# A fixed instruction order in one stage, y tiles split in place, and eight ordering edges on loads and weight splits in a decoder-layer kernel

## The chip, the cores and the metric

One core of a Trainium2 chip runs the kernel. The metric is device time in microseconds (us) from start to end of the program; the runs before the change gave 1829.06, 1829.22 and 1833.78, so their median is 1829.22. The engines are TensorE (PE; PEld is its weight load), VectorE (DVE), ScalarE (ACT), GpSimd (POOL) and SyncE (SP, which here issues nearly all loads).

## What is computed

One layer of a decoder trunk for a sequence of 1024 tokens and a width of 1024. Three kinds of head work side by side on the same normalized input, each is gated by a sigmoid of its own columns, the gated sum goes through W_out, and a feed-forward block with a short convolution follows. Cut to its core:

```python
h = rms_norm(x); P = h @ W_in
A = rwkv7(P)              # 8 heads x 64; per token: S = S*w + (S @ -kk)(kk*a) + v k ; y = S @ r
B = stick_breaking(P)     # 8 heads x 64, causal
M = cross_attention(P, mem)   # 4 heads x 128, 256 memory tokens
x += sum_b(sigmoid(G_b) * (branch_b @ W_br[b])) @ W_out
x += conv_ffn(rms_norm(x))
```

## The kernel before

**Numbers.** Every large product is made of three matmuls: each float32 operand is split into a high part that TensorE takes as it is and a low part (the rest), and `mm3` adds hi x hi, hi x lo and lo x hi into one PSUM bank. A weight tile of 128 x 1024 is loaded by SP into a `wr` slot (`load_w`, 2 slots), ACT copies it to `wh` (L81), and POOL subtracts to get `wl` (L82). The activations of a branch are split alike: `load_y` loads four 128 x 1024 tiles of branch output from DRAM (`yd`) into `w4` tiles, ACT writes `yhi` (L1129), DVE writes the low part into a tile of the tag `A` (L1130). The tag `w4` has 3 slots, and `A` has 4.

**Stages in time.** Input norm and transposes; the preparation of the recurrence (`rwkv_prep`); stick-breaking attention (`sb_attn`, 325 to 650 us); cross attention (`mem_attn`, to some 770 us); the recurrence (`stage2`, 805 to 1005 us) followed by its `group_norm`; the last branch (`branch_last`, to 1091 us); `out_proj`; and the feed-forward block, from 1187 us on.

**Two streams.** From the first preparation to the group norm, `weave` takes turns between a stage and a stream of items called the pump: projections of the input (`proj_item`: 8 steps of six matmuls into two PSUM banks of the tag `mm`, which has 4 banks) and products of a finished branch with its output weights (`branch_item`: 4 such steps). In the recurrence one step of `stage2` is followed by 2.08 steps of the pump. The pump does branch 1 (stick-breaking) in the first part of the recurrence and branch 2 (memory) in the second; between them stands one gate projection whose steps 3 to 6 call the four splits of `load_y`.

**A step of the recurrence.** `stage2` walks 16 chunks of 64 tokens, each in three steps. Step one multiplies the state and adds; DVE copies the result out of four `g` banks (`ys<-g`, L530, four copies). Step two solves; ACT copies eight results (`qk<-g`, L538). Step three makes the outputs and the new state; DVE updates the state (L548, four operations), ACT copies eight outputs (L550). The next step of the stage on PE needs these results, and its own banks. A part of the normalization (`norm_part`) is mixed in: sums on DVE (L573), squares on ACT (L580, `jk`), the scaling on DVE (L589).

**What sets the order.** A list scheduler orders each engine's instructions by their estimated readiness. `pinned` marks an instruction to be kept in program order among the marked ones of the whole program. Not marked before: the sums of `norm_part`, and the DVE operations that empty a branch item's banks (L1162), the copies that empty a projection's banks (L755, L797, L806) and the weight splits. SP issues its loads in one order, each waiting for its slot. At the end of a projection or a branch item `fin` or the emptying of banks comes in the same step as the last matmuls.

**The last branch.** `branch_last` loads for each of eight output tiles a gate (`at<-gsd`) and the sum so far (`w<-mrd`, L1198), and multiplies and adds on DVE (L1220, L1225). The eight weight tiles of W_out are loaded by `load_wo`, four within that loop, four behind it.

Of the kernel before, what the change touches and what calls it, by code (L numbers as in the profile page):

```python
# [50 lines left out]
class Trunk:  # L51
    def __init__(self, ctx, tc, I, out):
        self.ctx, self.tc, self.nc, self.I, self.out = ctx, tc, tc.nc, I, out
        self.uid = 0
        self.pin = False
# [19 lines left out]
    def load_w(self, src):  # L75
        raw = self.pool_wt.tile([128, 1024], F32, name=self.nm("wr"), tag="wr", bufs=2)
        self.nc.sync.dma_start(raw, src)
        return raw

    def split_raw(self, raw, hi, lo):  # L80
        self.nc.scalar.activation(hi, raw, AF.Copy)  # L81
        self.nc.gpsimd.tensor_tensor(lo, raw, hi.bitcast(F32), ALU.subtract)  # L82
        return hi, lo

# [23 lines left out]
    def pinned(self, ins):  # L108
        if self.pin:
            self.tc.keep_in_program_order(ins)  # L110

# [455 lines left out]
    def norm_part(self, g0, g1):  # L567
# [4 lines left out]
        for p, y in enumerate(ys):  # L572
            nc.vector.tensor_reduce(nm[:, p * nh : (p + 1) * nh], y.rearrange("p (g i) -> p g i", i=64), AX.X, ALU.add)  # L573
        nc.vector.tensor_scalar(nm[:, : 4 * nh], nm[:, : 4 * nh], -1.0 / 64, None, ALU.mult)
# [135 lines left out]
    def proj_item(self, src, fin, hook={}):  # L710
        w = self.split_w(src)
        yield
        out = [self.ps("mm"), self.ps("mm")]
        for k in range(8):
            ks = slice(k * 128, (k + 1) * 128)
            self.mm3(out, [a[:, ks] for a in w], self.xin(k), k == 0, k == 7)
            if k == 4:
                self.close_gates()
            if k in hook:
                hook[k]()  # L720
            if k < 7:
                yield
        fin(out)
        yield
# [24 lines left out]
    def gate_item(self, b, d, hook={}, keep=None):  # L749
        nc = self.nc  # L750

        def fin(pp):
            g = self.t4()
            for h in range(2):
                nc.scalar.activation(g[:, h * 512 : (h + 1) * 512], pp[h], AF.Copy)  # L755
# [13 lines left out]
    def sb_qk(self, p, out):  # L769
# [4 lines left out]
        def k_fin(pp):  # L774
            kr, sq = self.t4(), self.t4()
            for h in range(2):
                nc.scalar.activation(kr[:, h * 512 : (h + 1) * 512], pp[h], AF.Copy)
# [25 lines left out]
        def q_fin(pp):  # L803
            qr, sq = self.t4(), self.t4()
            for h in range(2):
                nc.scalar.activation(qr[:, h * 512 : (h + 1) * 512], pp[h], AF.Copy)  # L806
# [19 lines left out]
        hooks = {1: lambda: k_split(1), 3: q_ss, 4: lambda: q_split(0), 6: lambda: q_split(1)}  # L826
# [199 lines left out]
    def mem_q(self, h, out, hook):  # L1026
# [3 lines left out]
        def fin(pp):  # L1030
            sq = self.t4()
            qhi, qlo = self.t4("qk", F32R), self.t4("qk", F32R)
            for i in range(2):
                hs = slice(i * 512, (i + 1) * 512)
                self.pinned(nc.scalar.activation(qhi[:, hs], pp[i], AF.Copy, scale=self.par("memq")))
                self.pinned(nc.scalar.activation(sq[:, hs], pp[i], AF.Square))
# [74 lines left out]
    def load_y(self, b, st):  # L1111
# [4 lines left out]
        def load():  # L1116
            y = self.t4("w4")
            nc.sync.dma_start(y, self.yd[b, len(ys)])
            ys.append(y)

        def first():
            for _ in range(3):
                load()

        def split(k):
            if k == 0:
                st["hi"] = self.pool_a.tile([128, 4, 1024], F32R, name=self.nm("yhi"), tag="inst")
            hi, lo, y = st["hi"][:, k], self.t4("A", F32R), ys[k]
            self.pinned(nc.scalar.activation(hi, y, AF.Copy))  # L1129
            self.pinned(nc.vector.tensor_tensor(lo, y, hi.bitcast(F32), ALU.subtract))  # L1130
            out.append((hi, lo))
            if k == 0:
                load()
# [7 lines left out]
    def branch_item(self, b, d, st, first):  # L1141
# [11 lines left out]
        for k in range(4):  # L1153
# [3 lines left out]
            if k < 3:  # L1157
                yield
        g = st.pop(("g", d))
        for h in range(2):  # L1160
            hs = slice(h * 512, (h + 1) * 512)
            nc.vector.tensor_tensor(g[:, hs], pp[h], g[:, hs], ALU.mult)  # L1162
# [3 lines left out]
        yield  # L1166
# [11 lines left out]
    def load_wo(self, k):  # L1178
        slots = ["qk"] * 4 + ["at"] * 4 + ["it", "sp"] + ["qk"] * 4 + ["at"] * 2
        hl = [self.pool_l.tile([128, 1024], F32R, name="wo_sp", tag="sp", bufs=1) if s == "sp" else self.t4(s, F32R) for s in slots[2 * k : 2 * k + 2]]  # L1180
        self.wo.append(self.split_raw(self.load_w(self.I["w_out"][k]), *hl))

    def branch_last(self):
# [10 lines left out]
        def load(d):  # L1194
            if d < 8:
                go[d] = self.t4("at"), self.t4()
                nc.sync.dma_start(go[d][0], self.gsd[0, d])
                nc.sync.dma_start(go[d][1], self.mrd[d])  # L1198
# [587 lines left out]
    def run(self):  # L1786
# [62 lines left out]
        pace[0] = 8  # L1849
        need("sb0")  # L1850
# [3 lines left out]
        need("mem")  # L1854
        st2 = self.stage2()
        next(st2)
        need("y1")
        self.weave(st2, pump, 2.08, 0)
        self.weave(self.group_norm(), pump, 1.0, 0)
        drain(pump)  # L1860
# [80 lines left out]
```

## Time and profile before

| quantity | value |
|---|---|
| median of three runs | 1829.22 us |
| time of the profiled execution | 1831.78 us |
| its span, first to last instruction | 1830.0 us |
| PE busy | 1785.9 us |
| DVE / ACT / POOL busy | 1191.1 / 881.9 / 771.2 us |
| PE in 767 to 1025 us (recurrence) | 249.85 us of 258.00 |
| PE in 325 to 640 us (stick-breaking) | 310.85 us of 315.00 |

PE is busy nearly all of the time, so the table is to be read from what is missing on PE: the gaps between its instructions, and the stretches in which the profile shows a granted clock below 1. In the rows of a window view the columns are the window, its length, the busy time (and number of instructions) of PE, PEld, DVE, ACT and POOL, the granted clock, the share of the DMA engines that is busy, and GB/s. A row of waits says which engine and line waited for which, the sum in us, how many times, and the longest. A row of the timeline has the start, the time taken, the engine, the line, the operation and its tiles, and in brackets the idle time before it and what ended it. In the list of DMA issues the last number is the median time from issue to landing in us.

### The profile page before, as it was taken

What the parts mean: (1) busy time and instruction counts of PE and PEld (TensorE: products, weight loads), DVE (VectorE), ACT (ScalarE), POOL (GpSimd) and SP (SyncE); (2) the same over time, 40 slices, a digit from 0 to 9 for tenths busy, and PEclk for the clock granted to TensorE, in tenths of its full rate; (3) what the DMA queues carried; (4) which work ended last, traced back from release to release, by engine and by line L of the source; (5) the groups of instructions that cost most, each with busy time, mean ns of one, the idle gap of its engine ahead of it and who ended that gap; (6) DMA issues with size and microseconds to landing.
All of it is one profiled execution on the core that took longest, in us unless ns stands there. A gap on an engine that the chain in (4) does not pass through costs nothing.

```text
span 1830.0 us, 27430 instructions
## 1 busy us (share of the span) xinstructions
PE 1785.9 (98%) x10468; PEld 1445.7 (79%) x10468; DVE 1191.1 (65%) x1659; ACT 881.9 (48%) x1665; POOL 771.2 (42%) x441
## 2 busy tenths in 40 slices
PE   8999999999999999999899999989999999999999
PEld 6777778878788888787677878868888888888887
DVE  5657664988987514333444793597776777785497
ACT  5443342564666635534456443464454444545443
POOL 2322343232222452122233341376776767645454
PEclk9999999999999999999899999999999999999999
DMA  4255466111112351467665463323232232386475
GB/s 181 58 173 184 151 201 204 50 41 52 56 45 84 112 144 53 164 211 257 222 244 185 163 251 104 114 70 115 101 117 88 95 118 104 123 291 247 144 236 202
DMA packets 120613, 263.39 MB, mean 144 GB/s; under 512 B 28313, under 2 KB 40857, under 8 KB 120354
## 3 DMA queue, kind: packets, MB, share of 16 engines
q1 hardware_dynamic: 82722, 194.76, 32.6%
q10 hardware_dynamic: 33984, 54.27, 8.1%
q0 software_dynamic: 3776, 12.62, 2.2%
q8 instruction: 82, 1.34, 0.3%
q14 instruction: 49, 0.40, 0.1%
HBM read 180.04 MB, written 81.53 MB: 143 GB/s over the span
## 4 chain that ended last, share of the span: by engine, by line
PE 83%; DVE 8%; issue 3%; ACT 3%; POOL 2%; DMA 1%; ACTq 0%; SPq 0%; DVEq 0%; POOLq 0%
PE mm L113 67%; PE g L113 12%; PE g L106 3%; POOL dw L1677 1%; DVE qk L379 1%; DVE qk L381 1%; DVE it L462 1%; DVE BT L1318 1%; DVE inst L464 0%; DVE at L854 0%; DVE mg L1232 0%; DMA w<-yd 0%; ACT wh L81 0%; POOL wl L82 0%; DVE qk L382 0%
## 5 line engine op out<-in xcount | busy, mean ns | idle before, releaser
L82 POOL TENSOR_TENSOR wl<-wr,wh 128x1024 fp32r<-128x1024 f32 x77 | 196.8, 2557 | 473.4 <-ACT wh L81 469.7
L113 PE MATMUL mm<-xhi,wh 128*128 128x512 f32 x784 | 264.6, 418 | 9.4 <-ACT xhi L182 7.5
L113 PE MATMUL mm<-xlo,wh 128*128 128x512 f32 x784 | 245.8, 395 | 0.9 <-DVE xlo L183 0.9
L113 PE MATMUL mm<-xhi,wl 128*128 128x512 f32 x784 | 244.3, 393 | 0.3 <-POOL wl L82 0.2
L113 PEld LDWEIGHTS mm<-xlo,wh 128*128 128x128 f32 x784 | 148.8, 190 | 34.5 <-DVE xlo L183 1.6
L113 PEld LDWEIGHTS mm<-xhi,wl 128*128 128x128 f32 x784 | 148.3, 189 | 34.0 <-POOL wl L82 1.2
L113 PEld LDWEIGHTS mm<-xhi,wh 128*128 128x128 f32 x784 | 137.7, 191 | 39.5 <-issue 9.1
L81 ACT ACTIVATE wh<-wr 128x1024 fp32r<-128x1024 f32 x77 | 81.4, 1058 | 147.0 <-PE mm L113 85.4
L113 PE MATMUL mm<-dw,da 128*128 128x512 f32 x528 | 121.2, 390 | 0.0
L113 PE MATMUL mm<-BT,l 128*128 128x512 f32 x504 | 117.7, 390 | 0.0
L113 PEld LDWEIGHTS mm<-dw,da 128*128 128x128 f32 x528 | 99.0, 188 | 21.6 <-DVE da L1676 1.2
L1677 POOL TENSOR_TENSOR dw<-draw,dw 128x512 fp32r<-128x512 f32 x55 | 81.9, 1499 | 79.1 <-ACT dw L1675 76.4
L113 PE MATMUL mm<-BT,wh 128*128 128x512 f32 x352 | 109.2, 391 | 2.9 <-DVE BT L1318 2.9
L854 DVE TENSOR_TENSOR_SCAN at<-at,at 128x128 f32<-128x128 f32 (+3 forms) x64 | 93.4, 1460 | 26.6 <-ACT at L848 26.4
L113 PEld LDWEIGHTS mm<-BT,l 128*128 128x128 f32 x504 | 94.7, 188 | 19.6
L113 PE MATMUL mm<-B,wh 128*128 128x512 f32 x352 | 108.7, 390 | 1.5 <-DVE p L1508 1.5
L1676 DVE TENSOR_TENSOR da<-draw,da 128x512 fp32r<-128x512 f32 x77 | 67.0, 877 | 49.5 <-ACT da L1674 49.1
L1409 POOL TENSOR_TENSOR l<-it,l 128x1024 fp32r<-128x1024 f32 x21 | 51.6, 2458 | 95.5 <-ACT l L1408 95.5
L113 PE MATMUL g<-dw,da 128*128 128x512 f32 x396 | 90.6, 390 | 0.3 <-POOL dw L1677 0.3
L1674 ACT ACTIVATE da<-draw 128x512 fp32r<-128x512 f32 x77 | 48.3, 628 | 80.8 <-PE mm L113 30.9
L113 PEld LDWEIGHTS g<-dw,da 128*128 128x128 f32 x396 | 74.3, 188 | 16.1 <-POOL dw L1677 0.8
L756 DVE TENSOR_TENSOR w<-w,rbc 128x1024 f32<-128x1024 f32 x24 | 49.8, 2074 | 56.8 <-ACT w L755 55.0
(329 smaller groups left out, 3996.5 us busy)
## 6 DMA issues: line engine op xcount, KB each, us to landing
wr<-in_w_in_dram SPq DMA_DIRECT2D x50, 512.0 KB, 3.6
draw<-actd SPq DMA_DIRECT2D x77, 256.0 KB, 3.5
at<-scr SPq DMA_DIRECT2D x28, 512.0 KB, 5.8
draw<-in_w_down_dram SPq DMA_DIRECT2D x55, 256.0 KB, 4.7
rw<-in_w_up_dram SPq DMA_DIRECT2D x22, 512.0 KB, 3.5
actd<-gall ACTq DMA_DIRECT2D x44, 256.0 KB, 3.3
gsd<-w ACTq DMA_DIRECT2D x20, 512.0 KB, 2.8
wr<-in_w_up_dram SPq DMA_DIRECT2D x20, 512.0 KB, 3.6
```

What stands on the lines that cost most here:

```text
L81: self.nc.scalar.activation(hi, raw, AF.Copy)
L82: self.nc.gpsimd.tensor_tensor(lo, raw, hi.bitcast(F32), ALU.subtract)
L106: self.pinned(self.nc.tensor.transpose(out, in_, self.ident[:n, :n]))
L113: self.pinned(self.nc.tensor.matmul(*a, **k))
L379: nc.vector.tensor_tensor(bk4[q, :, first ^ h2], self.c8(x[q, hs]), self.c8(Q[q, hs]), ALU.mult)
L381: nc.vector.scalar_tensor_tensor(ra4[:, :, 1, 1:64], self.c8(P[:, hs])[:, :, 0:63], -1.0, self.c8(kk[:, hs])[:, :, 1:64], ALU.mult, ALU.mult)
L756: nc.vector.tensor_tensor(g, g, self.rbc, ALU.mult)
L854: self.pinned(nc.vector.tensor_tensor_scan(sn[:, :W][:, ::-1], sn[:, :W][:, ::-1], self.smask[:, 1024 - W :][:, ::-1], 1.0, ALU.mult, ALU. ...
L1409: keep(eng.tensor_tensor(lo, src, hi.bitcast(F32), ALU.subtract))
L1674: self.pinned(nc.scalar.activation(A[:, 0], a, AF.Copy))
L1676: self.pinned(nc.vector.tensor_tensor(A[:, 1], a, A[:, 0].bitcast(F32), ALU.subtract))
L1677: nc.gpsimd.tensor_tensor(Wt[:, 1], w, Wt[:, 0].bitcast(F32), ALU.subtract)
```

## The change

1. **`strict`**: while the recurrence and the group norm are woven with the pump, each pinned instruction gets an ordering edge to the pinned instruction before it on its engine. The sums of `norm_part` and the emptying of a branch item's banks (L1162) become pinned. `proj_item` and `branch_item` give up their turn after the last matmuls too, so that `fin` and the emptying are written one step later, behind the next step of the stage.
2. **`load_y`**: the four tiles are loaded straight into four `A` tiles, and all four loads are written at the start; ACT writes the high part, and DVE writes the low part over the tile itself. No `w4` slot is used.
3. **`load_wo`**: the last four loads of W_out on SP are ordered behind the last `mrd` load that has been issued by then.
4. **`guard`**: during stick-breaking and cross attention, ACT's weight copy (`wh`, L81) is ordered behind the last ACT copy out of the banks of the projection before it.
5. In the first head pair of stick-breaking, `q_ss` is called at step 2 of its projection and not at step 3.

```diff
+    def behind(self, ins, prev):
+        if prev is not None:
+            self.tc.add_manual_dep(ins.ins, prev.ins.name, ... NoSync ..., reason="fixed order")
     def pinned(self, ins):
         if self.pin:
             self.tc.keep_in_program_order(ins)
+            if self.strict:
+                self.behind(ins, self.last_fixed.get(ins.ins.engine))
+            self.last_fixed[ins.ins.engine] = ins
...
-    def load_w(self, src):
+    def load_w(self, src, after=None):
-        self.nc.sync.dma_start(raw, src)
+        self.behind(self.nc.sync.dma_start(raw, src), after)
...
-        self.nc.scalar.activation(hi, raw, AF.Copy)
+        ins = self.nc.scalar.activation(hi, raw, AF.Copy)
+        self.behind(ins, self.last_fin)
...
-            if k < 7:
+            if k < 7 or self.strict:
                 yield
         fin(out)
-        yield
+        if not self.strict:
+            yield
...
-            for _ in range(3):
-                load()
+            for k in range(4):
+                ys.append(self.t4("A", F32R))
+                nc.sync.dma_start(ys[k].bitcast(F32), self.yd[b, k])
...
-            hi, lo, y = st["hi"][:, k], self.t4("A", F32R), ys[k]
-            self.pinned(nc.scalar.activation(hi, y, AF.Copy))
-            self.pinned(nc.vector.tensor_tensor(lo, y, hi.bitcast(F32), ALU.subtract))
-            out.append((hi, lo))
-            if k == 0:
-                load()
+            hi, y = st["hi"][:, k], ys[k]
+            self.pinned(nc.scalar.activation(hi, y.bitcast(F32), AF.Copy))
+            self.pinned(nc.vector.tensor_tensor(y, y.bitcast(F32), hi.bitcast(F32), ALU.subtract))
+            out.append((hi, y))
...
-            if k < 3:
-                yield
+            yield
         g = st.pop(("g", d))
         for h in range(2):
-            nc.vector.tensor_tensor(g[:, hs], pp[h], g[:, hs], ALU.mult)
+            self.pinned(nc.vector.tensor_tensor(g[:, hs], pp[h], g[:, hs], ALU.mult))
...
-        self.wo.append(self.split_raw(self.load_w(self.I["w_out"][k]), *hl))
+        self.wo.append(self.split_raw(self.load_w(self.I["w_out"][k], self.last_go if k > 3 else None), *hl))
...
-                nc.sync.dma_start(go[d][1], self.mrd[d])
+                self.last_go = nc.sync.dma_start(go[d][1], self.mrd[d])
```

The order of matmuls on PE hardly changes (one step of six moves behind sixteen small ones in stick-breaking). The other engines' order changes at some places; the lines of the changed kernel are higher by 2 to 17. The first is ACT in the middle of the recurrence, where the gate projection between the two branches splits the y tiles. L550 (L567 in the changed kernel) are the output copies of a chunk, L580 (L597) the squares of the normalization, L1129 (L1143) the high part of a y tile. Before:

```order
L580 ACTIVATE jk_7687,hn_7536<-qk_6774,hn_7535 128x64
L550 ACTIVATE qk_6773<-g_7543 64x64
L580 ACTIVATE jk_7689,hn_7536<-qk_6774,hn_7535 128x64
L550 ACTIVATE qk_6773<-g_7543 64x64
L580 ACTIVATE jk_7691,hn_7536<-qk_6774,hn_7535 128x64
L1129 ACTIVATE yhi_7729<-w_1323_7611 128x1024
L550 ACTIVATE qk_6774<-g_7544 64x64
L580 ACTIVATE jk_7735,hn_7536<-qk_6775,hn_7535 128x64
L550 ACTIVATE qk_6774<-g_7544 64x64
L580 ACTIVATE jk_7737,hn_7536<-qk_6775,hn_7535 128x64
L550 ACTIVATE qk_6775<-g_7545 64x64
L580 ACTIVATE jk_7739,hn_7536<-qk_6775,hn_7535 128x64
```

And the same place on ACT in the changed kernel:

```order
L567 ACTIVATE qk_6773<-g_7541 64x64 x2
L597 ACTIVATE jk_7683,hn_7532<-qk_6772,hn_7531 128x64
L597 ACTIVATE jk_7685,hn_7532<-qk_6772,hn_7531 128x64
L597 ACTIVATE jk_7687,hn_7532<-qk_6772,hn_7531 128x64
L597 ACTIVATE jk_7689,hn_7532<-qk_6772,hn_7531 128x64
L1143 ACTIVATE yhi_7727<-A_7607 128x1024
L597 ACTIVATE jk_7730,hn_7532<-qk_6773,hn_7531 128x64
L597 ACTIVATE jk_7732,hn_7532<-qk_6773,hn_7531 128x64
L597 ACTIVATE jk_7734,hn_7532<-qk_6773,hn_7531 128x64
```

The copies out of the banks now come all ahead of the squares and of the first y split, where they took turns with them before.

The second is SP at the loads of branch 2's y tiles (`<-yd`; `at`, `qk` and `it` are the recurrence's own loads, `gsd` and `mrd` belong to branch items). Before:

```order
L496 DMA qk_7498<-td 128x256
L491 DMA at_7502<-scr 128x1024
L491 DMA at_7504<-scr 128x1024
L1118 DMA w_1324_7613<-yd 128x1024
L495 DMA qk_7506<-vd 64x256 x2
L496 DMA qk_7506<-td 128x256
L491 DMA it_7510<-scr 128x1024
L77 DMA wr_8146<-in_w_in_dram 128x1024
L1118 DMA w_1325_7615<-yd 128x1024
L1147 DMA w_1333_7667<-gsd 128x1024
L1150 DMA w_1334_7669<-mrd 128x1024
L1118 DMA w_1347_7733<-yd 128x1024
```

And in the changed kernel:

```order
L513 DMA qk_7494<-td 128x256
L1137 DMA A_7607<-yd 128x1024
L508 DMA at_7498<-scr 128x1024
L1137 DMA A_7609<-yd 128x1024
L508 DMA at_7500<-scr 128x1024
L1137 DMA A_7611<-yd 128x1024
L512 DMA qk_7502<-vd 64x256
L1137 DMA A_7613<-yd 128x1024
L512 DMA qk_7502<-vd 64x256
L513 DMA qk_7502<-td 128x256
L508 DMA it_7506<-scr 128x1024
L1162 DMA w_1331_7667<-mrd 128x1024
```

Before, the first y load stood three rows ahead of this piece and the last behind the `gsd` and `mrd` loads of the next item; now the four stand close together, ahead of that `mrd` load.

The third is DVE in the second half of the recurrence, where branch items empty their banks (`w<-mm`, L1162, L1173 in the changed kernel). L530 (L547) copies the result of step one, L589 (L606) scales, L548 (L565) updates the state, L573 (L590) sums. Before:

```order
L530 COPY ys_6776<-g_7999 128x64
L1162 TENSOR_TENSOR w_1368_7876<-mm_7974,w_1368_7876 128x512
L1162 TENSOR_TENSOR w_1368_7876<-mm_7975,w_1368_7876 128x512
L589 TENSOR_SCALAR qk_6774<-qk_6774,hn_7535,hf_7777 128x64 x4
L589 TENSOR_SCALAR qk_6775<-qk_6775,hn_7535,hf_7777 128x64 x4
L548 SCALAR_TENSOR_TENSOR ys_6776<-ys_6776,pc_90,g_7996 128x64
L548 SCALAR_TENSOR_TENSOR ys_6776<-ys_6776,pc_91,g_7997 128x64
L548 SCALAR_TENSOR_TENSOR ys_6776<-ys_6776,pc_92,g_7998 128x64
L573 TENSOR_REDUCE hn_8160<-qk_6772 128x4
L573 TENSOR_REDUCE hn_8160<-qk_6773 128x4
L573 TENSOR_REDUCE hn_8160<-qk_6774 128x4
L548 SCALAR_TENSOR_TENSOR ys_6776<-ys_6776,pc_93,g_7999 128x64
```

And in the changed kernel:

```order
L547 COPY ys_6774<-g_7991 128x64
L606 TENSOR_SCALAR qk_6772<-qk_6772,hn_7531,hf_7770 128x64 x4
L606 TENSOR_SCALAR qk_6773<-qk_6773,hn_7531,hf_7770 128x64 x4
L1173 TENSOR_TENSOR w_1360_7868<-mm_7966,w_1360_7868 128x512
L1173 TENSOR_TENSOR w_1360_7868<-mm_7967,w_1360_7868 128x512
L565 SCALAR_TENSOR_TENSOR ys_6774<-ys_6774,pc_90,g_7988 128x64
L565 SCALAR_TENSOR_TENSOR ys_6774<-ys_6774,pc_91,g_7989 128x64
L565 SCALAR_TENSOR_TENSOR ys_6774<-ys_6774,pc_92,g_7990 128x64
L565 SCALAR_TENSOR_TENSOR ys_6774<-ys_6774,pc_93,g_7991 128x64
L1173 TENSOR_TENSOR w_1367_7962<-mm_8056,w_1367_7962 128x512
L1173 TENSOR_TENSOR w_1367_7962<-mm_8057,w_1367_7962 128x512
L590 TENSOR_REDUCE hn_8152<-qk_6770 128x4
```

The emptying of the banks went from ahead of the scaling to behind it, and the sums from between the four state updates to behind them.

More of the change, by code (lines that the diff above doesn't have):

```diff
@@ L110, in pinned @@
             self.tc.keep_in_program_order(ins)
+            if self.strict:
+                self.behind(ins, self.last_fixed.get(ins.ins.engine))
+            self.last_fixed[ins.ins.engine] = ins
+        return ins
+    def behind(self, ins, prev):
+        if prev is not None:
+            self.tc.add_manual_dep(
+                ins.ins, prev.ins.name,
+                mybir.DependencyInfo(mybir.DependencyClass.NoSync, mybir.DependencyReason.DATA), reason="fixed order")
     def mmul(self, *a, **k):
@@ L1849, in run @@
         pace[0] = 8
+        self.guard = True
         need("sb0")
```

29 lines of the change are left out of this document (16 added, 13 removed).

## The prediction

> **What bounds the kernel now.** I read the page's busy times first, then its chain that ended last.
>
> ```profile
> PE 1785.9 (98%) x10468; PEld 1445.7 (79%) x10468; DVE 1191.1 (65%) x1659; ACT 881.9 (48%) x1665; POOL 771.2 (42%) x441
> PE 83%; DVE 8%; issue 3%; ACT 3%; POOL 2%; DMA 1%; ACTq 0%; SPq 0%; DVEq 0%; POOLq 0%
> ```
>
> PE is busy 98% of the span and is 83% of the chain. The change removes no matmul and hardly reorders any, so all that it can win is time in which PE stands still in the touched stages, or runs at a lower granted clock behind such a stop. It is some 44 us in the whole span, so the gain is small by nature. I went through the stages by windows, then listed PE's waits in each, and then asked for every wait what the engine waited for had been doing.
>
> ```profile
> 767.00:1025.00 258.00, 249.85 (x2288) 196.59 (x2286) 102.75 (x260) 125.99 (x431) 74.15 (x43) 0.98 0.64 220
> ```
>
> The recurrence has 8.15 us of standing PE and a mean clock of 0.98. Nearly all of that is in one place, the gate projection between branch 1 and branch 2:
>
> ```profile
> PE g L113 <- DVE ys L530: 4.1, 1, 4.1
> PE g L113 <- ACT qk L550: 2.6, 2, 1.7
> ```
>
> ```profile
> 868.97:873.30 4.33, 1.77 (x33) 1.25 (x32) 0.53 (x4) 3.66 (x16) 0.69 (x2) 0.96 1.01 287
> 873.30:876.40 3.10, 3.10 (x9) 2.48 (x8) 1.48 (x3) 0.00 (x0) 2.65 (x1) 0.50 0.50 204
> 889.60:894.10 4.50, 0.40 (x3) 0.01 (x1) 2.64 (x5) 1.87 (x4) 0.00 (x0) 0.93 0.96 348
> 894.10:900.30 6.20, 6.20 (x28) 4.73 (x28) 0.39 (x4) 2.64 (x9) 0.00 (x0) 0.50 0.59 228
> ```
>
> In the first window PE is idle for 4.33 - 1.77 = 2.56 us, in the third for 4.50 - 0.40 = 4.10. Behind each stands a window with a granted clock of 0.50 in which PE is busy all the time and does half the work: 3.10 and 6.20 us.
>
> **Term a, the copies on ACT.** The first stop waits for L550. These rows are ACT's:
>
> ```profile
> 869.05 0.34 ACT L580 ACTIVATE jk<-qk,hn 128x64 f32<-128x64 f32 x1
> 869.39 1.04 ACT L1129 ACTIVATE yhi<-w 128x1024 fp32r<-128x1024 f32 x1
> 870.45 0.22 ACT L550 ACTIVATE qk<-g 64x64 f32<-64x64 f32 x1
> 872.17 0.22 ACT L550 ACTIVATE qk<-g 64x64 f32<-64x64 f32 x1
> ```
>
> A y split of 1.04 us stands in the middle of the eight copies, and a square between every two: the last four copies take from 870.45 to 872.39. In the changed order all eight stand ahead of the squares and the split. Eight copies of 0.22 us are 1.8 us without anything between, so I take the whole stop as gone, 2.56 us. The slow clock behind it goes too: 3.10 us at half speed do 1.55 us of work, so 1.55 more. Term a is 4.1 us. The squares and the split come later by the copies; the norm's next use of them is one step of the recurrence away.
>
> A rule that speaks about this is in the Trainium skill, "TensorE: Matmul & The Clock Gate", Part 1: the clock falls to half after about 3.4 us of idle in a free-running window, so stops below some 3 us should not matter. By that rule the 1.55 us would have another cause than this stop, and the sum would be that much smaller; the trace does not agree, since the clock is 0.50 behind 2.56 us of idle in two pieces.
>
> **Term b, the last y load.** The second stop follows a chain, read from the chain of waits in that window:
>
> ```profile
> 883.43 5.71 DMA w<-yd
> 889.16 1.07 ACT yhi L1129
> 890.26 1.24 DVE A L1130
> 893.82 0.23 DVE ys L530
> ```
>
> ```profile
> 858.11 0.32 SPq L1118 DMA_DIRECT2D w<-yd  x1
> ...
> SPq L1118 <- DMA mrd<-w: 15.4, 3, 6.4
> ```
>
> (The first of these rows is the first y load's issue, from SP's timeline; the second is a row of SP's waits.)
>
> The fourth y tile is issued at 883.43 only, because SP sat 15.4 us at the three late y loads until a `w4` slot was free (a branch item's store from it had to land). ACT's split then waits for the landing, the low part on DVE behind it, and the state copies L530 stand behind that on DVE. With the loads in `A` tiles, no `w4` slot is needed. What they need is that branch 1's last low parts have been read:
>
> ```profile
> 863.90 0.63 PE L113 MATMUL mm<-yhi,wl 128*128 128x512 f32 x2
> w<-yd SPq DMA_DIRECT2D x4, 512.0 KB, 3.9
> at<-scr SPq DMA_DIRECT2D x7, 512.0 KB, 6.6
> ```
>
> PE's last product of branch 1 starts at 863.90, so the fourth load can be issued at some 864.5, 19 us earlier than now. The four y loads share the queue with `at` loads; by these rows' 3.9 and 6.6 us the first lands between 865 and 869, and if all four and three `at` tiles (3.5 MB) queue at the 413 GB/s to 204 GB/s of the neighbouring windows (I take 300), the last lands 12 us after 864.5, at 876.5. Its split starts at 889.16 now, and could not start before 883 with the others ahead of it, so there are some 6 us to spare. I take the whole stop and its slow window as gone: 4.10 + 6.20 / 2 = 7.2 us. The bounds are 0 (another load is late by as much) and 7.2.
>
> **Term c, the end of the recurrence.**
>
> ```profile
> PE g L113 <- DVE ys L530: 0.8, 1, 0.8
> PE g L113 <- ACT qk L550: 0.7, 1, 0.7
> 991.00 2.35 DVE L756 TENSOR_TENSOR w<-w,rbc 128x1024 f32<-128x1024 f32 x1
> 993.39 1.06 ACT L759 ACTIVATE w<-w 128x1024 f32<-128x1024 f32 x1 [1.05 <-DVE w L756]
> 998.54 1.29 DVE L1162 TENSOR_TENSOR w<-mm,w 128x512 f32<-128x512 f32 x2
> ```
>
> A sigmoid of 1.06 us stands ahead of the last two L550 copies, and the emptying of two banks (1.29 us) ahead of the fourth L530 copy. In the changed order both come behind all copies. Bounds 0 and 1.5; I take 1.2, because the product of 2.35 us ahead of the state update on DVE stays where it was.
>
> **Term d, the last branch.**
>
> ```profile
> PE mm L113 <- DVE at L1220: 1.5, 1, 1.5
> 1083.46 0.33 SPq L77 DMA_DIRECT2D wr<-in_w_out_dram  x1
> 1083.84 0.42 SPq L1197 DMA_DIRECT2D at<-gsd  x1
> 1088.40 1.29 DVE L1220 TENSOR_TENSOR at<-mm,at 128x512 f32<-128x512 f32 x2 [2.54 <-DMA at<-gsd]
> 1104.34 0.62 PE L113 MATMUL mm<-it,mg 128*128 128x512 f32 x2
> ```
>
> DVE waits 2.54 us for a gate tile that SP issued at 1083.84, behind three loads of W_out; PE's wait of 1.54 us for the next L1220 follows from it, since DVE works without a pause from there. With those loads behind the `mrd` loads the gate comes some 4 us earlier. I take 1.5 us (bounds 0 and 2). The price is that two W_out loads come up to 5 us later; the tile of the first is needed by PE at 1104.34, over 20 us later, so this is covered.
>
> **Term e, the weight splits behind the bank copies.**
>
> ```profile
> PE mm L113 <- ACT w L755: 0.8, 1, 0.8
> PE mm L113 <- ACT w L806: 0.7, 1, 0.7
> PE mm L113 <- DVE qk L1037: 1.2, 1, 1.2
> 387.60 1.06 ACT L81 ACTIVATE wh<-wr 128x1024 fp32r<-128x1024 f32 x1 [0.25 <-issue]
> 388.57 1.06 ACT L806 ACTIVATE w<-mm 128x512 f32<-128x512 f32 x2
> ```
>
> In each of the three places a weight split of 1.06 us runs just ahead of the copies that free the banks; the second pair of rows shows one. Turned round, the copies come 1 us earlier. That is 0.8 + 0.7 + 1.2 = 2.7 at most, and I take 2.3. The split comes 1 us later and POOL's low part with it; its user is the next item, which on PE is an item of 48 matmuls away, so this costs nothing while the order holds. The earlier `q_ss` moves no wait that the trace shows; 0, with 1 us either way.
>
> **Term f, what is late next.** The strict order adds waits: behind a y split that waits for its load, all copies on ACT wait; behind a bank's emptying, the state updates on DVE. No row shows such waits, since this order has not run. The nearest rows are the waits of terms c and e, 0.7 to 1.2 us each, so I take two of them, 2 us against the gain (bounds 0 and the rival below).
>
> **The sum** is 4.1 + 7.2 + 1.2 + 1.5 + 2.3 - 2.0 = 14.3 us. The profiled execution took 1831.78, so it would take 1817.5; the median is 2.56 us below that execution, which gives 1829.22 - 14.3 = 1814.9, and I predict 1815.
>
> **The rivals.**
>
> *The wait changes its name.* If the first y tile lands behind 869, ACT's split, and with the strict order everything behind it, waits; PE's stop is then for the same reason some 20 us earlier. For it speaks that the `A` loads stand behind an `at` load and wait for PE's last reads up to 864.5; before, the first was issued before 859. Against it speaks the slack of the first split, which is now behind eight copies and four squares. The price is most of term b: 1815 + 7 to 11 = 1822 to 1826.
>
> *Nothing gained.* PE's next limits take back what the stops gave, as in the attention, where the scan and the triangle on DVE would be late instead, or the order is not the one that decides. Terms c to e are then zero, and a and b are given back behind: 1825 to 1831.
>
> *Slower, through the emptying of the banks.* It now stands behind the scaling or the state updates of the next step:
>
> ```profile
> 909.00 1.29 DVE L1162 TENSOR_TENSOR w<-mm,w 128x512 f32<-128x512 f32 x2 [2.44 <-PE mm L113]
> 910.21 5.90 DVE L589 TENSOR_SCALAR qk<-qk,hn,hf 128x64 f32<-128x64 f32 x8
> 917.23 0.62 PE L113 MATMUL mm<-yhi,wh 128*128 128x512 f32 x2
> ```
>
> The banks emptied at 909.00 are written again at 917.23. With the scaling first, where it starts decides: at 909.0, where the emptying ran, it ends at 914.9, and 1.29 us later the banks are free, with 1 us to spare; if it can start only at 910.2, they are free at 917.4 and PE waits. The trace had the scaling run without a pause behind the emptying, so it was ready by then and probably before, and I hold the wait for unlikely. From a delay of more than some 5 us behind the end of an item on, PE waits at every item; fifteen pairs of banks by 1.3 us or more are 20 us, and the time is 1815 + 20 = 1835 or above.
>
> *The clock goes its own way.* If the half clock behind the first stop isn't caused by it, 1.55 us stay, and the time is 1816.5; a further slow window of 3 us somewhere else costs as much again.
>
> **How the numbers follow.** The forecast (1811 to 1818) has 0.58, the clock's own way 0.09 (1816 to 1819), the wait that changes its name 0.13, half of it above 1823.7, nothing gained 0.09, slower 0.11. A measurement of this kernel tells a difference of about 0.3% from none, 5.5 us: faster is below 1823.7, slower above 1834.7. So faster has 0.58 + 0.09 + 0.07 = 0.74, the same 0.06 + 0.09 = 0.15, slower 0.11. The range runs from 1808 (all terms at their upper bounds, f at zero, and 4 us of small gaps besides) to 1827 (the wait that changes its name, and 1 us more); the cases left out are slower and most of nothing gained.
>
> **What would show it.** Right: no PE wait for L530 (L547) or L550 (L567) of over 1 us between 860 and 900, a granted clock of 1 there, all four y loads issued by 866, DVE not waiting for a gate tile in the last branch, and the last branch starting some 13 us earlier. Wrong: a wait of ACT's y split for its load; PE waiting for `w<-mm` on DVE; or the same stops with other names behind them.

## The result and the profile after

The changed kernel takes 1825.33 us (median of nine runs, 1822.09 to 1826.17) against 1831.26 us for the kernel before (nine runs, 1829.06 to 1833.78). The ratio is 0.9963 with a 95% interval of 0.9955 to 0.9971: faster by 0.37%, some 7 us, where 14.3 us were forecast. The time lies in the range, and the direction is right; the gain is half of what was predicted. (One execution of after_again, further down, took 2528.99 us at a granted clock of 0.65; its ratio leaves it out.) The profiled execution took 1822.09 us, and its page begins like this:

```profile
span 1820.3 us, 27424 instructions
## 1 busy us (share of the span) xinstructions
PE 1784.4 (98%) x10468; PEld 1444.0 (79%) x10468; DVE 1191.1 (65%) x1659; ACT 882.7 (48%) x1665; POOL 770.1 (42%) x441
```

The busy times are those of before within 2 us; what has gone is time in which PE stood still or ran slowly. In the recurrence nearly all of it has gone, as the same window shows (PE 257.26 us of 258.00, clock 1.00; before, 249.85 and 0.98):

```profile
767.00:1025.00 258.00, 257.26 (x2344) 203.34 (x2342) 106.61 (x278) 132.12 (x445) 78.89 (x45) 1.00 0.62 217
```

On ACT, the eight copies L567 run together, the y split comes behind them, and SP has issued all four y loads by 867.1. These are rows of ACT's and of SP's timeline, and the one wait of PE that is left in the recurrence:

```profile
867.56 1.88 ACT L567 ACTIVATE qk<-g 64x64 f32<-64x64 f32 x8
...
871.10 1.04 ACT L1143 ACTIVATE yhi<-A 128x1024 fp32r<-128x1024 f32 x1
```

```profile
862.77 0.38 SPq L1137 DMA_DIRECT2D A<-yd  x1
...
866.51 0.54 SPq L1137 DMA_DIRECT2D A<-yd  x1
```

```profile
PE g L130 <- DVE ys L547: 0.5, 1, 0.5
```

The last branch is where it goes wrong. PE's wait for the emptying of the last banks, 1.5 us before, is now 2.3 us, and a stretch with a low granted clock stands behind it. The first row is from PE's waits, the others are windows:

```profile
PE mm L130 <- DVE at L1230: 2.3, 1, 2.3
```

```profile
1079.00:1083.50 4.50, 2.24 (x11) 1.54 (x9) 4.50 (x6) 1.31 (x4) 2.27 (x1) 1.00 0.67 164
1083.50:1088.00 4.50, 4.41 (x12) 3.25 (x13) 4.50 (x6) 2.02 (x3) 3.05 (x2) 0.63 0.17 69
```

And in cross attention there is a new wait, behind an exponential (first row). The second row is what is left of the wait of 1.2 us there, the third what is left of one of 0.7 us in stick-breaking:

```profile
PE g L130 <- ACT at L1091: 0.6, 1, 0.6
PE mm L130 <- DVE qk L1055: 0.5, 1, 0.5
PE mm L130 <- ACT w L824: 0.4, 1, 0.4
```

Matching PE's instructions one by one, the two profiles lie apart by: 0.3 us (changed kernel later) at the end of cross attention, -4.2 us behind the first stop of the recurrence, -10.3 behind the second, -11.6 at the end of the recurrence, -9.3 us behind the last branch, and -9.7 at the end. So terms a, b and c came, term e came to nothing, and term d came with the wrong sign.

**Two theories.** (a) What the prediction left out: a weight's low part is a subtraction on POOL, and while it runs, some DVE instructions do not. The edges of the change move these subtractions into chains of DVE for which PE waits. (b) The rival: the terms d and e are limited by what they wait for, loads and copies, and POOL has nothing to do with it.

These are the rows behind term d, of DVE and of POOL in the changed kernel:

```profile
1074.16 1.29 DVE L1230 TENSOR_TENSOR at<-mm,at 128x512 f32<-128x512 f32 x2 [1.29 <-PE mm L130]
1075.37 0.68 DVE L1242 TENSOR_TENSOR mg<-at,mg 128x512 fp32r<-128x512 f32 x1
1076.60 4.95 DVE L1242 TENSOR_TENSOR mg<-at,mg 128x256 fp32r<-128x256 f32 x2 [0.55 <-ACT mg L1241]
1081.47 1.28 DVE L1235 TENSOR_TENSOR at<-at,w 128x512 f32<-128x512 f32 x2
1082.68 1.28 DVE L1230 TENSOR_TENSOR at<-mm,at 128x512 f32<-128x512 f32 x2
```

```profile
1076.34 2.40 POOL L85 TENSOR_TENSOR wo_sp<-wr,it 128x1024 fp32r<-128x1024 f32 x1 [9.56 <-ACT it L83]
1078.70 2.56 POOL L85 TENSOR_TENSOR qk<-wr,qk 128x1024 fp32r<-128x1024 f32 x1
```

The wait of DVE for the gate tile is gone, as predicted: L1230 waits for PE at 1074.16, not for a load. But two L1242 of 128 x 256 take 4.95 us together, and in the same stretch, from 1076.34 to 1081.26, POOL makes two subtractions without a pause. One by one the two L1242 take 2.42 and 2.60 us; those of the tile before, from 1070.92 us on, took 0.41 us each. The chain of DVE is as late as before, and PE waits longer.

The same is seen in cross attention. Of the changed kernel, DVE and POOL:

```profile
692.83 1.94 DVE L1088 SCALAR_TENSOR_TENSOR nb<-mxt,hf 128x2 f32<-128x2 f32 x1
```

```profile
692.36 2.40 POOL L85 TENSOR_TENSOR wl<-wr,wh 128x1024 fp32r<-128x1024 f32 x1 [10.37 <-ACT wh L83]
```

And of the kernel before:

```profile
693.65 0.16 DVE L1070 SCALAR_TENSOR_TENSOR nb<-mxt,hf 128x2 f32<-128x2 f32 x1
```

```profile
690.10 2.40 POOL L82 TENSOR_TENSOR wl<-wr,wh 128x1024 fp32r<-128x1024 f32 x1 [9.37 <-ACT wh L81]
```

An operation on two columns took 1.94 us instead of 0.16, because the subtraction, 2.3 us later than before through the ordering of the weight copy, ran beside it. The exponential behind it came late, and PE with it.

The Trainium skill has this: "SBUF — State Buffer", Terms, says that DVE and GpSimd share one pair of ports to SBUF, which one of them holds for a whole instruction while the other stands still, and "GPSIMD Engine Reference", Specifications, names DVE instructions with two inputs in SBUF among those that meet it. These rows agree: L1242 and L1088 have two inputs there. Two L1220 of the kernel before, with one input in PSUM, took no longer than elsewhere (1.29 us from 1088.40) though POOL subtracted from 1088.85 to 1091.25. The prediction weighed no such rule.

### The profile page after: what moved, and what is told of

It reads as the page before. It is cut to its first block, busy times and chain, and to the rows that moved or that the text cites. A ratio compares the mean times of both kernels' runs of the same rounds, so it can differ in the third digit from the quotient of the medians.

```text
span 1820.3 us, 27424 instructions
## 1 busy us (share of the span) xinstructions
PE 1784.4 (98%) x10468; PEld 1444.0 (79%) x10468; DVE 1191.1 (65%) x1659; ACT 882.7 (48%) x1665; POOL 770.1 (42%) x441
## 4 chain that ended last, share of the span: by engine, by line
PE 77%; DVE 12%; issue 4%; ACT 3%; POOL 2%; DMA 2%; ACTq 0%; SPq 0%; DVEq 0%; POOLq 0%
PE mm L130 63%; PE g L130 11%; PE g L113 3%; POOL dw L1687 1%; DVE it L479 1%; DVE at L872 1%; DVE inst L481 1%; DVE qk L396 1%; DVE qk L398 1%; DVE BT L1328 1%; DVE w L774 0%; DVE qk L819 0%; DVE at L1235 0%; DMA w<-mrd 0%; DVE qk L606 0%
## 5 line engine op out<-in xcount | busy, mean ns | idle before, releaser
L186 POOL TENSOR_TENSOR hf<-rs,half 128x16 f32<-128x16 f32 (+1 forms) x18 | 48.9, 2718 | 91.1 <-DVE rs L183 86.4
```

Source lines behind the costliest of these rows:

```text
L186: nc.gpsimd.tensor_tensor(out, t[:, :n], self.half[:, :n], ALU.pow)
```

## The experiments

All are timed in five rounds against the kernel before on the same chip; it had medians of 1831.42, 1831.99 and 1831.11 us in the three groups of four below. The first column says what a kernel holds.

| run | kernel | median us | ratio to before (95%) |
|---|---|---|---|
| after_again | the changed kernel | 1824.27 | 0.9958 (0.9944 to 0.9971) |
| after_nowo | it, without the W_out edges | 1821.92 | 0.9944 (0.9932 to 0.9957) |
| after_noguard | it, without the ordering of weight copies | 1823.67 | 0.9957 (0.9943 to 0.9971) |
| after_wodve | it, two subtractions moved to DVE | 1824.11 | 0.9962 (0.9949 to 0.9974) |
| only_y | before, with y tiles in place | 1826.62 | 0.9969 (0.9958 to 0.9981) |
| only_strict | before, with the strict order | 1826.47 | 0.9970 (0.9959 to 0.9981) |
| wodve2 | changed, two subtractions on DVE behind the chain | 1820.26 | 0.9928 (0.9915 to 0.9940) |
| best1 | wodve2, weight copies ordered in stick-breaking only | 1818.76 | 0.9925 (0.9912 to 0.9937) |
| y_strict | changed, without W_out edges and ordering | 1820.97 | 0.9947 (0.9934 to 0.9959) |
| only_wo | before, with the W_out edges | 1835.07 | 1.0018 (1.0009 to 1.0027) |
| only_guard | before, with the ordering of weight copies | 1832.93 | 1.0009 (1.0000 to 1.0018) |
| nowo_dve | wodve2, without the W_out edges | 1818.58 | 0.9932 (0.9920 to 0.9945) |

**The changed kernel again (after_again), unchanged.**

> The changed kernel once more, for a second profile and a longer series. Its first profile was 3 us shorter than the median of the runs. If that difference is a stop or a slow-clock window that comes and goes, the second profile shows one more of them (1.5 to 3 us) somewhere; if the stages differ everywhere by a little, none can be named. Theory (a): GpSimd's weight low parts hold VectorE, so PE waits again some 2.3 us for L1230 near 1081 us. Median expected 1825, 6 us under the kernel before.

1824.27 us. The wait for L1230 came again:

```profile
PE mm L130 <- DVE at L1230: 2.8, 1, 2.8
```

The second profile is as short as the first (span 1821.0), so it shows no further stop; what lies between these profiles and the median of the runs is left to the last section.

**Without the W_out edges (after_nowo).**

```diff
-self.load_w(self.I["w_out"][k], self.last_go if k > 3 else None)
+self.load_w(self.I["w_out"][k], None)
```

> The changed kernel without the edges on the four W_out loads. Theory (a), these edges put two weight splits of GpSimd side by side into VectorE's chain of the last branch: without them PE's wait for L1230 falls from 2.3 to about 1.5 us and the slow clock behind it may go too, so 0.8 to 2.5 us faster than the changed kernel, 1822.5 to 1824.5. Rival (b), the edges do bring the gate tile earlier and save what they were priced at: 1.5 us slower, 1826.5 or above.

1821.92 us, some 2 us less than after_again, as theory (a) has it; but the two intervals overlap, so the times alone do not settle it. The wait is that of before again:

```profile
PE mm L130 <- DVE at L1230: 1.5, 1, 1.5
```

The rival's 1826.5 lies outside this run's interval. A low clock still stands behind this wait in this profile, so I had hoped for too much there.

**Without the ordering of weight copies (after_noguard).**

```diff
-        self.guard = True
+        self.guard = False
```

> The changed kernel without the ordering of the weight copies behind the bank copies in the two attentions. Theory (a), the later weight split moves GpSimd's low part into VectorE's softmax chain and gives back what it saves: within 1 us of the changed kernel, 1824.5 to 1826, and at about 693 us the small VectorE operation of L1088 takes 0.16 us instead of 1.94. Rival (b), the ordering is worth the 2.3 us it was priced at: 1827.5.

1823.67 us, within 1 us of after_again. The three waits of 0.8, 0.7 and 1.2 us are back, and the small operation takes 0.16 us, with the subtraction ahead of it. The rival's 1827.5 lies outside the interval, which ends at 1826.1. DVE's and POOL's rows:

```profile
693.13 0.16 DVE L1088 SCALAR_TENSOR_TENSOR nb<-mxt,hf 128x2 f32<-128x2 f32 x1
```

```profile
689.59 2.40 POOL L85 TENSOR_TENSOR wl<-wr,wh 128x1024 fp32r<-128x1024 f32 x1 [9.37 <-ACT wh L83]
```

**Two subtractions on DVE (after_wodve, then wodve2).** The low parts of the W_out tiles k = 4 and 5, those that ran at 1076.34 and 1078.70 on POOL, are made on DVE.

```diff
-        self.nc.gpsimd.tensor_tensor(lo, raw, hi.bitcast(F32), ALU.subtract)
+        (low or self.nc.gpsimd).tensor_tensor(lo, raw, hi.bitcast(F32), ALU.subtract)
...
+    low = self.nc.vector if k in (4, 5) else None
```

> The changed kernel, where the low parts of two W_out tiles (k = 4 and 5) are subtracted on VectorE and not on GpSimd, everything else the same. Theory (a), GpSimd holds VectorE: the two L1242 of 2.4 and 2.6 us take 0.41 us again, the two subtractions add 1.2 us each, so the chain is 2 us shorter and PE's wait for L1230 falls from 2.3 us to 0.5 or less, and the slow clock behind it goes: 2 to 3 us faster than the changed kernel, 1822 to 1823. Rival (b), the gate tile's landing sets it: the wait stays at 2.3 or grows by 2.4, 1825 to 1828.

1824.11 us, no faster than after_again, and PE's wait is 2.5 us. So the expectation failed; the wait is as rival (b) has it, but not for the gate tile. The rows of DVE say why the run didn't test what it was meant to:

```profile
1077.78 1.22 DVE L85 TENSOR_TENSOR wo_sp<-wr,it 128x1024 fp32r<-128x1024 f32 x1 [3.72 <-ACT it L83]
1078.93 1.28 DVE L1230 TENSOR_TENSOR at<-mm,at 128x512 f32<-128x512 f32 x2
1080.12 1.36 DVE L1242 TENSOR_TENSOR mg<-at,mg 128x512 fp32r<-128x512 f32 x3
```

The three L1242 take 1.36 us together, as theory (a) has it, but the scheduler had put the subtraction ahead of L1230, where DVE waited 3.72 us for the high part from ACT. One wait took the other's place. In wodve2 the two subtractions are ordered behind the last L1242 of the last branch:

```diff
+        if low:
+            self.behind(ins, self.last_low)
...
+        self.last_low = rest.pop(0)()
```

> The changed kernel, where the low parts of the W_out tiles k = 4 and 5 are subtracted on VectorE behind the last subtraction of the last branch, and not on GpSimd. Theory (a), GpSimd's two subtractions held VectorE: the chain of L1230, L1242 and L1235 runs at its own pace, VectorE reaches the last L1230 when PE has just ended that tile, PE's wait falls from 2.3 us to 0.5 or less, and no slow clock follows: 2.5 to 3.3 us faster than the changed kernel, 1821.5 to 1822.5. Rival (b), a load or ACT sets the chain: PE's wait stays above 1.5 us and the time within 1 us of the changed kernel.

1820.26 us, 4 us less than after_again (5.5 by the ratios), with intervals that do not touch. PE has no wait in the last branch and the out projection's start, and the clock stays at 1; the windows that had 2.24 of 4.50 us and a clock of 0.63 are:

```profile
1079.00:1083.50 4.50, 4.50 (x22) 3.72 (x21) 2.79 (x6) 3.95 (x7) 0.00 (x0) 1.00 0.56 227
1083.50:1088.00 4.50, 4.50 (x21) 3.48 (x20) 4.40 (x10) 1.33 (x3) 0.00 (x0) 1.00 0.00 0
```

```profile
1080.70 0.76 DVE L1244 TENSOR_TENSOR mg<-at,mg 128x256 fp32r<-128x256 f32 x2 [1.98 <-ACT mg L1243]
...
1087.72 1.22 DVE L85 TENSOR_TENSOR wo_sp<-wr,it 128x1024 fp32r<-128x1024 f32 x1
1088.86 1.22 DVE L85 TENSOR_TENSOR qk<-wr,qk 128x1024 fp32r<-128x1024 f32 x1
```

The pair of 128 x 256 takes 0.76 us where it took 4.95, with POOL at rest. Theory (b) falls for term d.

**With the ordering in stick-breaking only (best1).**

```diff
         need("kv")
+        self.guard, self.last_fin = False, None
```

> As the run before, and the ordering of weight copies only in stick-breaking, not in cross attention. Theory (a), in cross attention that ordering moves GpSimd's subtraction beside VectorE's small L1088 and costs 0.6 us on balance: a further 0.6 us, 1821 to 1822. Rival (b), it is worth what it was priced at there (1.2 us): 1 us slower than the run before.

1818.76 us, 1.5 us less than wodve2 by the medians and 0.5 by the ratios, with intervals that overlap almost wholly, so the times tell neither theory from the other. In the profiles, cross attention is 0.5 us shorter than in wodve2, close to the 0.6 of theory (a).

**The parts alone.** In-place y tiles alone:

> The kernel before with the in-place y tiles alone. Theory (a): the second stop (4.1 us for L530 behind the last y load, and 6.2 us at half clock) goes, the first (L550) stays as it was, since ACT's order is the scheduler's as before: 6 to 7 us faster than the kernel before, some 1824.5. Rival (b), the late load only moves the wait to another engine or place: 0 to 3 us faster, 1828 to 1831.

1826.62 us, 5.4 us less than the kernel before. The interval, 3.5 to 7.7 us, holds theory (a)'s 6 to 7 and leaves out the 0 to 3 of (b). The strict order alone, with `load_y`, W_out loads and weight copies as before:

> The kernel before with the strict order and the later emptying of banks alone (y tiles through w4 as before, no edges on W_out loads, no ordering of weight copies). Theory (a): the copies L550 come together, so the first stop and its slow clock go (4 us), and the waits at the end of the recurrence (1.2 us); the late y load still stops PE at some 890 us: 4 to 6 us faster than the kernel before, 1826 to 1827. Rival (b), the strict order makes the wait for the y load worse, since ACT's copies stand behind the y split: 0 to 2 us, 1829 to 1831.

1826.47 us, 5.5 us less, as theory (a) expects. But the windows show that the two parts do not keep to the terms. The first two rows are of only_y, the others of only_strict:

```profile
868.00:873.00 5.00, 2.46 (x20) 1.63 (x18) 0.00 (x0) 4.83 (x24) 1.96 (x2) 1.00 1.02 396
873.00:877.00 4.00, 3.96 (x29) 3.24 (x30) 1.93 (x6) 0.32 (x2) 2.93 (x1) 0.69 1.04 410
```

```profile
868.00:873.00 5.00, 5.00 (x68) 4.04 (x63) 1.60 (x9) 4.73 (x20) 2.91 (x2) 1.00 1.01 371
884.00:892.00 8.00, 5.79 (x62) 4.34 (x63) 3.54 (x11) 4.95 (x12) 2.40 (x1) 1.00 0.90 321
892.00:897.00 5.00, 4.01 (x32) 2.73 (x32) 1.21 (x1) 2.81 (x9) 0.00 (x0) 1.00 0.88 329
```

With the y tiles alone, the first stop stays whole (2.54 us idle, and a mean clock of 0.69 in the 4 us behind it), and at the second place a wait of 1.4 us for L530 is left. With the strict order alone the first stop is gone, and at the second place PE still loses 2.21 + 0.99 us, but in pieces of 1.0 us or less with the clock at 1, where before it lost 4.10 at once and ran 6.20 us at half. ACT's split waits 2.8 us for its load there and the copies behind it wait too, as rival (b) has it, at a smaller price. By PE's instructions only_strict wins 2.0 us at this place and only_y 5.5, of the 6.1 that the changed kernel wins. So a part of term b goes with the order of DVE and ACT too, not only with the earlier load.

**Both, without the rest (y_strict).** It has the two edits of after_nowo and after_noguard.

> The changed kernel without the edges on the W_out loads and without the ordering of weight copies, so in essence the strict order and the in-place y tiles. If the parts add up, it has the 5.4 and 5.5 us of the two runs with one part alone: 11 us faster than the kernel before (theory a), 1820.5 to 1821.5, and so faster than the whole change. Rival (b), the two parts get the same microseconds twice: 7 to 8 us faster, 1824, as the whole change.

1820.97 us, 10.1 us less than before, and 2 to 4 us less than the whole change, by ratios and by medians, though the intervals overlap a little. The parts add up nearly, as in theory (a); the interval of 7.5 to 12.1 us leaves rival (b) its lower edge. By PE's instructions the recurrence is 11.9 us shorter, against 5.4 and 7.5 in the two runs alone, so that they share about 1 us.

**The other two parts alone.**

> The kernel before with the edges on the four W_out loads alone. Theory (a), the gate tile's wait goes but two subtractions of GpSimd stand side by side against VectorE's chain: PE's wait for the last bank emptying of the last branch grows from 1.5 to 2.3 us or more and a slow clock follows it: 1 to 2 us slower than the kernel before. Rival (b), as it was priced: 1.5 us faster.

1835.07 us: 3.3 to 4.0 us slower than before by ratio and medians, an interval of 0.09% to 0.27%. The wait for the last emptying is 2.5 us instead of 1.5:

```profile
PE mm L119 <- DVE at L1226: 2.5, 1, 2.5
```

Theory (a) has the sign and the wait, and the price is even higher than it said: 2.6 us of it lie in the last branch, where the pair of 128 x 256 takes 4.95 us again. The ordering of the weight copies:

> The kernel before with the ordering of weight copies behind bank copies in the two attentions alone. Theory (a): 0 to 0.7 us faster, no more than the runs can tell; the three waits of 0.8, 0.7 and 1.2 us fall to 0.4 or less, 0.4 and 0.5, and a wait for L1073 (exponentials of cross attention) of 0.6 us comes up. Rival (b), as it was priced: 2.3 us faster.

1832.93 us, slower by 0.09% with an interval from 0.00% to 0.18%: not faster, so the rival's 2.3 us are left out, and theory (a)'s gain too. The waits fell as expected, and the new one is there; in this profile a slow clock follows it, while the same wait in the changed kernel has a clock of 1.00 behind it:

```profile
PE g L125 <- ACT at L1085: 0.6, 1, 0.6
PE mm L125 <- DVE qk L1049: 0.5, 1, 0.5
PE mm L125 <- ACT w L818: 0.4, 1, 0.4
```

```profile
699.00:704.00 5.00, 5.00 (x18) 4.08 (x18) 3.08 (x11) 2.45 (x9) 2.68 (x4) 0.66 0.12 41
```

**Are the W_out edges of any use once POOL is out of the way (nowo_dve)?**

```diff
-self.load_w(self.I["w_out"][k], self.last_go if k > 3 else None)
+self.load_w(self.I["w_out"][k], None)
```

> The changed kernel without the edges on the W_out loads, and with the low parts of the tiles k = 4 and 5 on VectorE behind the last subtraction of the last branch. It tells whether the edges are of use once GpSimd is out of the way. Theory (a): VectorE still waits 2.5 us for the gate tile, of which the chain, 0.9 us shorter, leaves PE a wait of 0.5 us: 1 us slower than the kernel with both, 1820.5 to 1821.5. Rival (b), the gate's landing does not matter: the same as with both.

1818.58 us, ratio 0.9932 against 0.9928 for wodve2: no difference that can be told, and PE has no wait there in either. The expected wait for the gate did not come up, so the run does not test what it was meant to. SP's rows say why: the gate is issued early without any edge, and the last two W_out loads come 13 us behind it, since the slots of the two before them are held until the late subtractions have read them.

```profile
1073.27 0.32 SPq L1209 DMA_DIRECT2D at<-gsd  x1
1074.48 0.33 SPq L1276 DMA_DIRECT2D w<-in_x_dram  x1
1086.93 1.50 SPq L79 DMA_DIRECT2D wr<-in_w_out_dram  x2
```

So with the subtractions on DVE the edges show no use. Whether the late gate or the held DVE caused the wait of the kernel before is not settled by it. There both stood in the chain, as these rows show (the same three L1232 with POOL at rest until the third, and behind the gate):

```profile
1071.57 1.34 DVE L1232 TENSOR_TENSOR mg<-at,mg 128x512 fp32r<-128x512 f32 x3
...
1089.61 2.86 DVE L1232 TENSOR_TENSOR mg<-at,mg 128x512 fp32r<-128x512 f32 x3
```

2.54 us for the gate and 1.5 us for the subtraction, of which either is as long as PE's wait of 1.5.

## Why the prediction was off by half

**What bounds the kernel**: right. What the change won and lost is PE's idle time and slow clock. By PE's instructions the stages gained, in us, in the profiled executions (a minus is a loss):

| term, stage | priced | changed kernel | y_strict | wodve2 |
|---|---|---|---|---|
| a, first stop | 4.1 | 4.6 | 4.6 | 4.6 |
| b, second stop | 7.2 | 6.1 | 6.2 | 6.1 |
| c, end of the recurrence | 1.2 | 1.3 | 1.3 | 1.4 |
| d, last branch | 1.5 | -2.3 | -0.1 | 2.0 |
| e, 300 us to the end of cross attention | 2.3 | -0.5 | 0.2 | -0.6 |

(y_strict has neither the edges of d nor the ordering of e; wodve2 has both, and the two subtractions on DVE.)

**Terms a, b and c**, 12.5 us: right in mechanism and nearly in size, 12.0 us. The copies run together, the loads come by 867.1, and no wait above 0.5 us is left in the recurrence. Term a's slow clock went with its stop, against the rule of the Trainium skill that the prediction set beside it. The split of causes was not quite right: only_strict shows that a part of the second stop goes with the order as well. Of term f's 2.0 us of new waits no profile shows any.

**Term d**, a gain of 1.5 us: this step failed, and its sign with it. "With those loads behind the `mrd` loads the gate comes some 4 us earlier" held as far as DVE did not wait for it, and "so this is covered" was wrong. I priced the moved loads by the product on PE that needs the tile, over 20 us later. What a moved load also moves is everything that follows it: ACT's copy and POOL's subtraction. Two loads that SP issued 2.8 us apart (1076.41 and 1079.21) were now issued 0.4 us apart, and two subtractions that had started at 1081.03 and 1088.85 now stood side by side, 2.40 and 2.56 us long, just where DVE's chain was the one that PE waited for. wodve2, which takes only these two off POOL, takes 4 us off the changed kernel. The step is off by some 4 us: 1.5 were forecast as gained, and the last branch lost 2.3 here and 2.6 in only_wo.

**Term e**, a gain of 2.3 us: failed in the same step: the split "comes 1 us later and POOL's low part with it; its user is the next item ..., so this costs nothing". The three waits fell by 0.8 (none is listed there any more), 0.3 and 0.7 us, 1.8 of their 2.7, and POOL's later subtraction held L1088 for 1.8 us and gave back 0.6. That is not all. Up to 600 us the changed kernel wins 1.3 us; then comes a stretch at half clock, 3.4 us from 617 us on, which takes 1.6 us back. Six of the eight profiles with the ordering in stick-breaking have it, only_guard has one behind its new wait instead, and none of the six without the ordering has either. By only_guard the term is a cost of 0 to 3 us; its executions have a mean granted clock of 0.9945 against 0.9954 for the kernel before, which is worth 1.6 of the 1.8 us between the medians. Why the ordering brings slow stretches is open.

Terms d and e together were priced at +3.8 us. They came to -2.8 in the changed kernel's profile, and to some -5 or -6 in the two runs with one of them alone. The profile is 9.7 us shorter than the one before; that the medians and the ratio give only 6 to 7 us is the matter of the last section. The fifth edit, priced at 0, was not run alone; in y_strict, which has it, 300 to 420 us is 0.2 us shorter than before.

**The rivals.** None of them was this one. The place where I looked for a slower kernel, the later emptying of banks, showed no wait for it in any profile. "The wait that changes its name" did not come about either, since the y loads landed in time. It is what the upper part of the range stood for, so that the time lies in the range is luck. The nearest was "PE's next limits take back what the stops gave", but it named the scan, not POOL. And the signs by which the prediction was to be known as right came about nearly all (no such waits, the clock at 1, the y loads by 867, no wait for the gate tile, the last branch 12 us earlier); none of them was about what the moved work would meet.

## What to carry to other kernels

When an edge or a wait moves a load or a copy, follow the whole chain that hangs on it, and ask of each link on GpSimd what VectorE does at its new place: in these traces an operation of GpSimd of 2.4 us made a hole of some 2 us in VectorE where its next instruction had two inputs in SBUF. Price an edit at nothing only when both are looked up, its consumer and its neighbours. And test the parts of a change alone: here two of four parts held all of the gain, and the two others cost some of it.

## What the runs showed of the hardware

A granted clock of 0.63 or 0.66 in a window is a mean. In all 14 profiles a slow stretch within the span is a clock of 0.50 for 3.41 us, or twice that, which the windows above cut at other places. The stop of 2.3 us in the changed kernel shows it:

```profile
1081.24:1084.65 3.41, 1.15 (x4) 0.74 (x5) 3.41 (x7) 2.27 (x4) 0.14 (x2) 1.00 0.69 202
1084.65:1088.06 3.41, 3.41 (x10) 2.67 (x9) 3.41 (x4) 1.07 (x2) 3.00 (x2) 0.50 0.00 0
1088.06:1091.47 3.41, 3.41 (x17) 2.81 (x16) 3.41 (x3) 1.24 (x3) 2.20 (x1) 1.00 0.01 2
```

So each costs PE 1.7 us of work, and the stretches behind the two stops of the prediction, 3.41 and 6.83 us long, cost 1.7 and 3.4 us and not 1.55 and 3.1. Within a profile these stretches start whole steps of 3.413 us apart: in the kernel before at 152.75, 309.77, 872.97 and 893.45 us, which is 46, 165 and 6 steps. Whether one follows a stop depends on how much of a single step it fills. In the 14 profiles, from some 15 us on, each of the 29 steps in which PE stood idle for 1.9 us or more was followed by a slow one; of the 33 steps with 1.6 to 1.8 us only 13 were, and of those with less nearly none. So the same wait of 1.5 us in the last branch has no slow stretch behind it in the kernel before and in y_strict, and has one in only_strict. The exceptions, with little or no idle time ahead of a slow stretch, are the second step behind the second stop, the one at 699 us in only_guard, and those at some 310 and 617 us, where PE is listed as busy with 64 matmuls of one to four columns; what counts there is not shown.

And slow stretches come and go where nothing is changed: from 103 to 108 us, ahead of all edits, the kernel before has the first of these rows, and only_guard the second, which costs it 1.6 us.

```profile
103.00:108.00 5.00, 5.00 (x26) 4.16 (x26) 3.07 (x7) 3.35 (x4) 3.56 (x2) 1.00 0.76 262
```

```profile
103.00:108.00 5.00, 4.39 (x17) 3.59 (x18) 3.55 (x7) 2.31 (x4) 2.58 (x2) 0.71 0.61 216
```

Several such places make 2 to 3 us between executions of one kernel. That explains why both profiles of the changed kernel, at 1822, lie below its median of 1825: of its nine executions the three of 1822.1 to 1823.9 us have a mean granted clock of 0.996, and the six of 1825.2 to 1826.2 one of 0.995, and one stretch of 3.41 us at half clock is 0.001 of the span. None of the six was profiled, so where their stretches lie is not known.
